# Value products of the grouped-query attention: from column-tiled fp32 matmuls to full-array one-pass matmuls with split operands

## The chip, the cores and the metric

The kernel runs on one core of one Trainium2 chip. The metric is the device time of one execution in microseconds. Lower is better. Three runs of the kernel before gave 1745.05 to 1748.7 us, with a median of 1747.95 us.

## The reference, cut to what matters

One inference step of a two-layer trunk for 512 latent and 128 context tokens of width 1024. Layer 1 is grouped-query attention: 16 query heads, 4 key/value heads of width 64. Latent queries read 512 latent and 128 cached context keys in one softmax, and context queries read the 128 context keys alone.

```python
def one(qblk):
    s = jnp.einsum('bhgqd,bhkd->bhgqk', qblk, k).astype(jnp.float32) * scale
    p = jax.nn.softmax(s, axis=-1).astype(v.dtype)
    return jnp.einsum('bhgqk,bhkd->bhgqd', p, v)
...
k_all = jnp.concatenate([k, k_ctx], axis=2)
v_all = jnp.concatenate([v, v_ctx], axis=2)
o = block_attention(q.reshape(b, GQA_KV_HEADS, GQA_GROUP, n, HEAD_DIM), k_all, v_all)
```

The change concerns the last einsum, p times v.

## The kernel before, in words

Activations lie feature-major: 8 tiles of 128 features by 640 tokens (`NT`, latents first). The big products are made in float32r, a one-pass format of TensorE: each operand is split into a high part (a rounding copy on ACT) and a low part (source minus high part, on DVE or POOL, function `split`), and three matmuls, low-high, high-low and high-high, add up in PSUM (`step`, line 153, tile `mm`). Weights come through `weights` (tiles `ws`, then `wh` and `wl`, lines 111 and 112). `helper` picks DVE or POOL for the subtraction: a table `WPOOL` says, by stage, that every n-th goes to POOL. It held `mix0` alone, so in the stage `mix1`, which is layer 1's attention, all weight splits were DVE's.

`layer1` is that stage. After the k and q projections of the first heads, `tokens_major` makes v with tokens on partitions (tile `tm` in PSUM, copied to `v` by ACT and DVE in turn), and then `pipeline` runs over 72 units: for each of 8 head pairs m, four blocks of 128 queries times two heads e, and one unit for the context queries (`context_unit`, tiles with `ctx` in the name). A unit of `units_of` has these steps:

- scores: four float32r matmuls of 320 columns into tile `gs` (lines 1259 and 1260)
- exps (in `soft`): row maximum on DVE (`mx`, 1011), times the query's norm `rq` (1013), exponential with sum on ACT (1017, tile `gp`)
- norm (in `soft`): reciprocal and product with it on DVE (1022, 1025)
- turn: five transposes of 128 by 128 on TensorE into two PSUM banks (`gpt`, 1268)
- gather: copies of the two banks to SBUF, 256 columns on DVE (1272) and 384 on ACT (1273), tile `gpy`
- values, once for both heads of a pair: ten fp32 matmuls into tile `gpo` (1279), head 0 to PSUM partitions 0 to 63 and head 1 to 64 to 127, then one ACT copy to `gao` (1281)

A step's lag sets how far it runs behind: norm and turn one unit behind the scores, gather and values two. Behind each step `fill.some(rate)` lays matmuls of the q projections of later heads and, from m = 5, of the first half of the output projection, so TensorE has work while a softmax runs. The engines run their own queues in order; the order in them is set by the framework's scheduler from a timeline of its own, with the attention's steps ahead in priority.

## Time and profile before

| what | us |
|---|---|
| median of three runs | 1747.95 |
| the profiled execution | 1748.81 |
| its span, first to last instruction | 1747.0 |
| TensorE busy, of the span | 1672.7 |
| VectorE busy | 1277.5 |
| ScalarE busy | 722.8 |
| GpSimd busy | 206.2 |
| the attention units, first maximum to the last value products | 985 to 1222 |

The profiled execution lasts 1.8 us longer than its span, and 0.9 us longer than the median. Busy time of an engine counts each moment once. In the trace an fp32 matmul or transpose may show as more than one record, and neighbours on one engine overlap a little, since the next starts before the last has written.

### The profile page before, as it was taken

To read this page: it belongs to the slowest core of one execution; us is meant where nothing else is said; L and a number is where in the kernel's file an instruction comes from. 1 tells how busy PE (TensorE), PEld (TensorE's weight loads), DVE (VectorE), ACT (ScalarE), POOL (GpSimd) and SP (SyncE) were. 2 spreads that over 40 slices of the span, in tenths; PEclk is the share of its full clock that TensorE was granted. 3 is DMA by queue.
4 is the path that set the end of the run, shared out by engine and by line. 5 is a ranking of instruction groups with operands and counts; after the bars stand their busy time and mean duration, and the time that the engine had idled before them with its cause. 6 is when DMAs were issued, how large, how long until landed. Compare 5 with 4: busy or idle time off the path is not lost.

```text
span 1747.0 us, 33431 instructions
## 1 busy us (share of the span) xinstructions
PE 1672.7 (96%) x13142; PEld 1573.8 (90%) x13142; DVE 1277.5 (73%) x2877; ACT 722.8 (41%) x1599; POOL 206.2 (12%) x475
## 2 busy tenths in 40 slices
PE   8978899989999999999999999999999999999997
PEld 6867777879899999999998788878899999999997
DVE  5899954765899989997557988875775644663654
ACT  4443254454533322332335566754453322331342
POOL 2134441310200000000003311000110000000001
PEclk8988998999999999999999999999999999999998
DMA  8623223233154555444232200110212222222222
GB/s 314 207 91 130 98 86 99 80 101 97 55 175 155 159 169 183 148 149 131 69 120 89 66 20 19 35 67 22 73 61 74 85 73 73 73 66 93 72 64 72
DMA packets 68014, 175.22 MB, mean 100 GB/s; under 512 B 7920, under 2 KB 9744, under 8 KB 66832
## 3 DMA queue, kind: packets, MB, share of 16 engines
q1 hardware_dynamic: 67024, 171.48, 30.2%
q8 instruction: 103, 1.69, 0.4%
q0 software_dynamic: 832, 1.60, 0.3%
q14 instruction: 55, 0.45, 0.1%
HBM read 165.71 MB, written 7.34 MB: 99 GB/s over the span
## 4 chain that ended last, share of the span: by engine, by line
PE 81%; DVE 12%; DMA 3%; ACT 2%; issue 2%; POOL 0%; SPq 0%; ACTq 0%; DVEq 0%; POOLq 0%
PE mm L153 65%; PE gpo L1279 3%; PE gpt L1268 2%; DVE junk L316 1%; DVE wa L316 1%; PE gs L1259 1%; DMA wa<-in_ada_wt_dram 1%; DVE wl L112 1%; PE gs L1260 1%; PE napo L1076 1%; DVE eb L847 1%; PE ss L410 1%; PE go L949 1%; DVE ea L841 1%; DMA x<-in_xT_dram 1%
## 5 line engine op out<-in xcount | busy, mean ns | idle before, releaser
L153 PE MATMUL mm<-hh,wl 128*128 128x320 f32 x2080 | 651.7, 315 | 5.3 <-DVE x L488 1.0
L153 PE MATMUL mm<-hl,wh 128*128 128x320 f32 x2080 | 648.4, 312 | 0.0
L153 PE MATMUL mm<-hh,wh 128*128 128x320 f32 x2080 | 642.0, 312 | 0.0
L111 ACT CAST wh<-ws 128x512 fp32r<-128x512 f32 x376 | 228.8, 615 | 443.0 <-PE mm L153 404.0
L153 PEld LDWEIGHTS mm<-hh,wl 128*128 128x128 f32 x2080 | 394.6, 190 | 15.6 <-issue 5.9
L153 PEld LDWEIGHTS mm<-hl,wh 128*128 128x128 f32 x2080 | 395.4, 190 | 2.9 <-DVE h L445 1.2
L153 PEld LDWEIGHTS mm<-hh,wh 128*128 128x128 f32 x2080 | 393.3, 190 | 0.9 <-issue 0.3
L112 DVE TENSOR_TENSOR wl<-ws,wh 128x512 fp32r<-128x512 f32 x348 | 240.2, 693 | 159.3 <-ACT wh L111 158.4
L153 PE MATMUL mm<-glo,wh 128*128 128x320 f32 x704 | 217.0, 309 | 0.0
L153 PE MATMUL mm<-ghi,wh 128*128 128x320 f32 x704 | 216.7, 309 | 0.0
L153 PE MATMUL mm<-ghi,wl 128*128 128x320 f32 x704 | 215.8, 309 | 0.0
L488 DVE SCALAR_TENSOR_TENSOR x<-mm,mod,x 128x192 f32<-128x192 f32 (+2 forms) x240 | 96.8, 435 | 93.4 <-PE mm L153 92.6
L153 PEld LDWEIGHTS mm<-ghi,wl 128*128 128x128 f32 x704 | 131.7, 188 | 0.9 <-issue 0.9
L153 PEld LDWEIGHTS mm<-glo,wh 128*128 128x128 f32 x704 | 132.2, 188 | 0.0
L153 PEld LDWEIGHTS mm<-ghi,wh 128*128 128x128 f32 x704 | 132.0, 188 | 0.1
L316 DVE SCALAR_TENSOR_TENSOR junk<-wa,sb 128x512 f32<-128x512 f32 x160 | 115.6, 727 | 7.5 <-DMA wa<-in_ada_wt_dram 7.2
L316 DVE SCALAR_TENSOR_TENSOR wa<-wa,sb 128x512 f32<-128x512 f32 x160 | 117.7, 742 | 0.3
L522 POOL MEMSET u<- 128x1 f32 x88 | 8.9, 103 | 766.3 <-DVE gate L515 432.3
L525 ACT COPY u<-mm 128x320 f32<-128x320 f32 x88 | 37.8, 432 | 88.0 <-PE mm L153 83.1
L592 PE MATMUL tm<-wl,hh 128*128 128x256 f32 x200 | 58.6, 297 | 9.8 <-ACT v L601 7.0
L1011 DVE TENSOR_REDUCE mx<-gs 128x1 f32<-128x640 f32 x64 | 52.5, 821 | 16.6 <-PE gs L1260 16.0
L1017 ACT ACTIVATE gp<-gs,mx,rq 128x640 f32<-128x640 f32 x64 | 57.1, 892 | 9.5 <-DVE mx L1013 5.1
(302 smaller groups left out, 2480.7 us busy)
## 6 DMA issues: line engine op xcount, KB each, us to landing
ws<-in_wu_dram SPq DMA_DIRECT2D x88, 512.0 KB, 3.2
wa<-in_ada_wt_dram SPq DMA_DIRECT2D x160, 256.0 KB, 3.3
ws<-in_wd_dram SPq DMA_DIRECT2D x32, 448.0 KB, 3.2
aw<-in_ada_w_dram SPq DMA_DIRECT2D x8, 1024.0 KB, 15.7
ws<-in_w_ab_dram SPq DMA_DIRECT2D x16, 512.0 KB, 4.2
ws<-in_wd_dram SPq DMA_DIRECT2D x16, 512.0 KB, 3.7
x<-in_xT_dram SPq DMA_DIRECT2D x16, 320.0 KB, 5.5
ws<-in_w_gqa_dram SPq DMA_DIRECT2D x10, 512.0 KB, 3.9
```

The source lines that it names most:

```text
L111: nc.scalar.copy(hi, src)
L112: eng.tensor_tensor(lo, src, hi, ALU.subtract)
L153: nc.tensor.matmul(ps, x, y[:, s], start=st, stop=sp_)
L316: nc.vector.scalar_tensor_tensor(w if v else junk, w, 1.0, cs[v, j], ALU.mult, ALU.mult, accum_out=acc[:, k, v, j:j + 1])
L410: nc.tensor.matmul(ps[0:rows, c:c + 2], part[:, t], onesd, start=True, stop=True)
L488: nc.vector.scalar_tensor_tensor(x[:, b:e], ps[:, b - HN * h:e - HN * h], gate[:, v, m:m + 1], old[:, b:e], ALU.mult, ALU.add)
L525: nc.scalar.copy(u[:, 1:321], ps)
L592: nc.tensor.matmul(ps, hh[:, s], wlo, start=(k == 0), stop=False)
L1011: nc.vector.tensor_reduce(mx[:, 0:n], s, axis, ALU.max, negate=True)
L1017: nc.scalar.activation(dst, src, AF.Exp, bias=mx[:, i:i + 1], accum_out=sm[:, i:i + 1], **kw)
L1268: nc.tensor.transpose(dst, u["p"][0][:, 128 * t:128 * t + 128], ident)
L1279: nc.tensor.matmul(po[64 * f:64 * f + 64, 0:128], vs[t][:, 64 * kv:64 * kv + 64], mates[f]["x"][:, 128 * t:128 * t + 128], start=(t == 0), ...
```

## The change

The value products become float32r matmuls on the whole array. Each token tile of v is kept as high and low part side by side (`gvs`, 64 columns each, so one key/value head is a stationary operand of 128 columns). The transposed probabilities of both heads of a pair are split into high (`hi`, two ACT copies per unit) and low (`lo`, two DVE subtractions per unit). For each of five token tiles two matmuls of 256 columns, 128 for each head, add into one bank: rows 0 to 63 hold the high part of v times p, rows 64 to 127 the low part. A new helper, `weighted`, copies the lower half out on ACT (`gpl`) and adds it to the upper half with two DVE additions. The product with the reciprocal (norm) moves from DVE to POOL for the latent units. `WPOOL` gives POOL every second weight split of `mix1`. Buffers: `gpy` holds one pair instead of two, `ctxp` one unit in this stage, and `adarow` and `kx` move to another pool.

```diff
+                if take:
+                    take(t, ps)
+                    yield
+                    continue
...
-                kx = sp.tile([P, CTX], F32, tag="kx", name="kx")
+                kx = T("kx", "kx", n=CTX, bufs=2)
...
-                nc.vector.tensor_scalar_mul(w, w, sm[:, i:i + 1])
+                (scaler or nc.vector).tensor_scalar_mul(w, w, sm[:, i:i + 1])
...
+        def take(t, src):
+            w = T("gvs", "gvs", F32R, n=512, bufs=6)
+            hi, lo = (w.rearrange("p (g i d) -> p i g d", g=4, i=2)[:, i] for i in range(2))
+            src = src.rearrange("p (g d) -> p g d", g=4)
+            nc.scalar.copy(hi, src)
+            nc.vector.tensor_tensor(lo, src, hi, ALU.subtract)
+            vs.append(w.rearrange("p (g n) -> p g n", g=4))
...
+        def weighted(ot, s, kv, pairs):
+
+            po = P1("gpo", "po")[:, 0:256]
+            n = len(pairs)
+            for t, (v, hi, lo) in enumerate(pairs):
+                nc.tensor.matmul(po, v[:, kv, :], lo, start=(t == 0), stop=False)
+                nc.tensor.matmul(po, v[:, kv, :], hi, start=False, stop=(t == n - 1))
+            low = T("gpl", "gpl", n=256, bufs=1)[0:64]
+            nc.scalar.copy(low, po[64:128])
+            for e in range(2):
+                c = slice(128 * e, 128 * e + 128)
+                nc.vector.tensor_tensor(ot[64 * e:64 * e + 64, s], po[0:64, c], low[:, c], ALU.add)
...
                 def gather():
-                    u["x"] = y = T("gpy", "gpy", bufs=4)
-                    nc.vector.tensor_copy(y[:, 0:256], u["pt"][0][:, 0:256])
-                    nc.scalar.copy(y[:, 256:640], u["pt"][1][:, 0:384])
+                    if e == 0:
+                        u["x"] = [T("gpy", "gpy", F32R, n=2 * NT, bufs=2).rearrange("p (e n) -> p e n", e=2) for _ in range(2)]
+                    hi, lo = (y[:, e] for y in mates[0]["x"])
+                    for w, pt in ((slice(0, 256), u["pt"][0][:, 0:256]), (slice(256, 640), u["pt"][1][:, 0:384])):
+                        nc.scalar.copy(hi[:, w], pt)
+                        nc.vector.tensor_tensor(lo[:, w], pt, hi[:, w], ALU.subtract)
...
-                    for t in range(5):
-                        for f in range(2):
-                            nc.tensor.matmul(po[64 * f:64 * f + 64, 0:128], vs[t][:, 64 * kv:64 * kv + 64],
-                                             mates[f]["x"][:, 128 * t:128 * t + 128], start=(t == 0), stop=(t == 4))
-                    nc.scalar.copy(ot[:, s], po[:, 0:128])
+                    hi, lo = mates[0]["x"]
+                    cols = [slice(128 * t, 128 * t + 128) for t in range(5)]
+                    weighted(ot, s, kv, [(vs[t], hi[:, :, c], lo[:, :, c]) for t, c in enumerate(cols)])
...
-WPOOL = {'mix0': 2}
+WPOOL = {'mix0': 2, 'mix1': 2}
```

TensorE's queue at the value products of the 27th of the 32 pairs, in the kernel before (`gpt` is a transpose, `gpo` a value product, `gs` scores, `gvc` the cached values):

```order
L1279 MATMUL gpo<-gpy,v 64x128
L1268 MATMUL gpt<-ident,gp 128x128
L1279 MATMUL gpo<-gpy,v 64x128
L1268 MATMUL gpt<-ident,gp 128x128
L1279 MATMUL gpo<-gpy,v 64x128 x3
L1259 MATMUL gs<-gkk,q 128x320
L1260 MATMUL gs<-gkl,q 128x320
L1259 MATMUL gs<-gkk,q 128x320
L1260 MATMUL gs<-gkl,q 128x320
L1268 MATMUL gpt<-ident,gp 128x128 x3
L1279 MATMUL gpo<-gpy,v 64x128 x3
L1279 MATMUL gpo<-gpy,gvc 64x128 x2
```

The same pair in the kernel with the change (1271 is a product with the low part of p, 1272 with the high part, 1303 a transpose; two more products follow):

```order
L1271 MATMUL gpo<-gpy,gvs 128x256
L1303 MATMUL gpt<-ident,gp 128x128
L1272 MATMUL gpo<-gpy,gvs 128x256
L1303 MATMUL gpt<-ident,gp 128x128
L1271 MATMUL gpo<-gpy,gvs 128x256
L1272 MATMUL gpo<-gpy,gvs 128x256
L1303 MATMUL gpt<-ident,gp 128x128 x2
L1271 MATMUL gpo<-gpy,gvs 128x256
L1303 MATMUL gpt<-ident,gp 128x128
L1272 MATMUL gpo<-gpy,gvs 128x256
L1271 MATMUL gpo<-gpy,gvs 128x256
L1272 MATMUL gpo<-gpy,gvs 128x256
```

The value products still stand among the transposes of the next unit, but all of them now use 128 columns of the array instead of 64, and each streams 256 columns.

DVE's queue late in the attention, in the kernel before (`mx` is the maximum, `sm` the reciprocal, `x` a residual of the output projection):

```order
L1272 COPY gpy<-gpt 128x256
L1022 RECIPROCAL sm<-sm 128x1
L1025 TENSOR_SCALAR gp<-gp,sm 128x640
L1011 TENSOR_REDUCE mx<-gs 128x1
L1013 TENSOR_TENSOR mx<-mx,rq 128x1
L1011 TENSOR_REDUCE mx<-gs 128x1
L1272 COPY gpy<-gpt 128x256
L1022 RECIPROCAL sm<-sm 128x1
L1013 TENSOR_TENSOR mx<-mx,rq 128x1
```

The same stretch with the change (1311 is a subtraction of gather, 1277 an addition of `weighted`, 1015, 1017 and 1026 the lines 1011, 1013 and 1022 of before):

```order
L1026 RECIPROCAL sm<-sm 128x1
L1017 TENSOR_TENSOR mx<-mx,rq 128x1
L1015 TENSOR_REDUCE mx<-gs 128x1
L1017 TENSOR_TENSOR mx<-mx,rq 128x1
L1026 RECIPROCAL sm<-sm 128x1
L1311 TENSOR_TENSOR gpy<-gpt,gpy 128x256
L1311 TENSOR_TENSOR gpy<-gpt,gpy 128x384
L1015 TENSOR_REDUCE mx<-gs 128x1
L1277 TENSOR_TENSOR gao<-gpo,gpl 64x128 x2
```

The product with the reciprocal is gone from DVE (it stands in POOL's queue now), so a reciprocal, which releases POOL, is followed at once by other DVE work, here by the small product `mx`; two subtractions stand where a copy stood.

## Rows read from the trace of the kernel before

**Rows 1.** The page: the span, and each engine's busy time in it.

```profile
span 1747.0 us, 33431 instructions
...
PE 1672.7 (96%) x13142; PEld 1573.8 (90%) x13142; DVE 1277.5 (73%) x2877; ACT 722.8 (41%) x1599; POOL 206.2 (12%) x475
```

**Rows 2.** Windows over the attention: us, each engine's busy us, clock, DMA share, GB/s.

```profile
1102.00:1142.00 40.00, 40.00 (x362) 32.95 (x361) 34.88 (x93) 27.01 (x65) 6.41 (x4) 1.00 0.20 65
...
1182.00:1222.00 40.00, 40.00 (x298) 32.20 (x298) 22.08 (x59) 16.86 (x42) 0.00 (x0) 1.00 0.06 21
sum 237.00, PE 233.62 PEld 196.07 DVE 189.56 ACT 145.98 POOL 23.36; mean PE 38.94 PEld 32.68 DVE 31.59 ACT 24.33 POOL 3.89
```

**Rows 3.** The chain that ended last, 985 to 1222 us, by line.

```profile
by line: PE mm L153 28.6%; PE gpo L1279 22.9%; PE gpt L1268 17.3%; PE gs L1259 8.9%; PE gs L1260 7.1%; DVE mx L1011 1.7%; DMA ws<-in_w_gqa_dram 1.4%; PE gst L1175 1.3%; PE ctxo L1116 1.1%; DVE wl L112 1.1%; PE ctxpt L1107 1.0%; issue 0.9%; 
```

**Rows 4.** Timeline of TensorE: start, us. Value products in one piece.

```profile
1087.80 0.31 PE L153 MATMUL mm<-hh,wh 128*128 128x320 f32 x1
1088.04 1.09 PE L1279 MATMUL gpo<-gpy,v 128*64 128x128 f32 x16
...
1089.29 0.55 PE L1268 MATMUL gpt<-ident,gp 128*128 128x128 f32 x3
```

**Rows 5.** Timeline of TensorE: value products broken up by transposes.

```profile
1101.60 0.27 PE L1268 MATMUL gpt<-ident,gp 128*128 128x128 f32 x1
1101.81 0.65 PE L1279 MATMUL gpo<-gpy,v 128*64 128x128 f32 x6
...
1104.07 0.42 PE L1259 MATMUL gs<-gkk,q 128*128 128x320 f32 x1
```

**Rows 6.** Timeline of TensorE: float32r matmuls of 256 columns, first and 14th of a run.

```profile
965.81 0.28 PE L593 MATMUL tm<-wh,hl 128*128 128x256 f32 x1
...
967.34 0.28 PE L594 MATMUL tm<-wh,hh 128*128 128x256 f32 x1
```

**Rows 7.** Longest waits, 985 to 1222 us: who, for whom, us, times, longest.

```profile
PEld gpt L1268 <- issue: 8.6, 50, 0.2
PEld gpo L1279 <- issue: 8.1, 46, 0.2
```

**Rows 8.** Groups of DVE by shape, 985 to 1222 us: busy, mean ns, idle before.

```profile
L1025 DVE TENSOR_SCALAR gp<-gp,sm 128x640 f32<-128x640 f32 x64 | 36.3, 568 | 0.4
L1272 DVE COPY gpy<-gpt 128x256 f32<-128x256 f32 x64 | 26.7, 417 | 12.5 <-PE gpt L1268 12.0
L112 DVE TENSOR_TENSOR wl<-ws,wh 128x512 fp32r<-128x512 f32 x24 | 17.4, 734 | 1.1 <-ACT wh L111 1.0
L1013 DVE TENSOR_TENSOR mx<-mx,rq 128x1 f32<-128x1 f32 x64 | 14.1, 221 | 0.2
...
L488 DVE SCALAR_TENSOR_TENSOR x<-mm,mod,x 128x320 f32<-128x320 f32 x7 | 3.8, 547 | 2.1 <-PE mm L153 2.1
...
L488 DVE SCALAR_TENSOR_TENSOR x<-mm,mod,x 128x128 f32<-128x128 f32 x6 | 2.1, 342 | 0.0
...
L1013 DVE TENSOR_TENSOR mx<-mx,rq 128x2 f32<-128x2 f32 x8 | 1.2, 154 | 0.1
```

**Rows 9.** Timeline of POOL and DVE: start, us.

```profile
1088.06 1.72 POOL L1181 TENSOR_TENSOR gx<-gx,cosT 128x512 f32<-128x512 f32 x1
1088.57 1.23 DVE L1013 TENSOR_TENSOR mx<-mx,rq 128x1 f32<-128x1 f32 x1
```

**Rows 10.** Groups of POOL by shape, whole span.

```profile
L701 POOL CAST kl<-kl 64x320 fp32r<-64x320 f32 x16 | 8.2, 514 | 25.9 <-DVE kl L699 25.4
...
L941 POOL TENSOR_TENSOR qd<-qd,kqg 128x640 f32<-128x640 f32 x4 | 6.1, 1545 | 7.4 <-ACT qd L830 7.4
```

**Rows 11.** Groups of ACT by shape, 985 to 1222 us.

```profile
L1111 ACT COPY ctxx<-ctxpt 128x256 f32<-128x256 f32 x8 | 3.0, 378 | 3.9 <-PE ctxpt L1107 3.9
```

**Rows 12.** Windows of the first conv FFN, where DVE is busiest; columns as in Rows 2.

```profile
680.00:720.00 40.00, 40.00 (x275) 40.00 (x274) 39.09 (x95) 14.81 (x34) 1.12 (x15) 1.00 0.52 169
...
sum 240.00, PE 239.42 PEld 239.16 DVE 224.51 ACT 73.93 POOL 4.41; mean PE 39.90 PEld 39.86 DVE 37.42 ACT 12.32 POOL 0.73
```

More of the change, by code (lines that the diff above doesn't have):

```diff
@@ L286, in spread_modulation @@
             nc.tensor.matmul(ps[j:j + 32, 0:128 * n], siluc[:, r, :], w[:, 128 * n * r:128 * n * (r + 1)], start=(r < 4), stop=(r >= 4))
-        row = sp.tile([P, 256], F32, tag="adarow", name="adarow")[:, 0:128 * n]
+        row = T("adarow", "adarow", n=256, bufs=2)[:, 0:128 * n]
         nc.scalar.copy(row, ps[:, 0:128 * n])
@@ L575, in conv_ffn, with tokens_major @@
         return into_norm(xs, gate(), lambda done: run(products(ws[0:KD - 3], g, done, kinds, n)), ws, g, n, final=final)
-    def tokens_major(src, n, H, vs, tag, bufs=None, out=None):
+    def tokens_major(src, n, H, vs, tag, bufs=None, out=None, take=None):
         per = 512 // n
-        for t in range(5):
+        for t in range(0 if take else 5):
             if t % per == 0:
@@ L1119, in view @@
         def view():
-            t = T("ctxp", "ctxp", n=256, bufs=2)
+            t = T("ctxp", "ctxp", n=256, bufs=1 if scale is not None else 2)
             return [t[:, 0:128], t[:, 128:256]]
@@ L1236, in layer1, with latents @@
         together([a["w_gqa"][c] for c in range(3)], H, kq_done, make)
-        v = []
-        run(tokens_major(a["w_gv"], 256, H, v, "gv", 3))
-        nc.gpsimd.dma_start(o["gqa_v"], v[4][:, 0:256])
+        vs = []
+        def take(t, src):
[5 more added lines that the diff above has]
+            vs.append(w.rearrange("p (g n) -> p g n", g=4))
+        def latents(t, ps):
+            take(t, ps)
+            if t == 4:
+                x = T("gvc", "gvc", n=256, bufs=1)
+                nc.scalar.copy(x, ps)
+                nc.gpsimd.dma_start(o["gqa_v"], x)
+        run(tokens_major(a["w_gv"], 256, H, None, None, take=latents))
         vc = T("gvc", "gvc", n=256, bufs=1)
         nc.sync.dma_start(vc, a["gqa_vc"])
-        vs = v[0:4] + [vc]
+        take(None, vc)
+        vx = vs.pop(4)
         outs = []
+        def weighted(ot, s, kv, pairs):
[9 more added lines that the diff above has]
+                nc.vector.tensor_tensor(ot[64 * e:64 * e + 64, s], po[0:64, c], low[:, c], ALU.add)
         def units_of(m, q, r):
@@ L1291, in units_of, with gather @@
                 units += [unit(b, e, mates) for e in range(2)]
-            units.append(context_unit(q, [KX[kv]] * 2, [KXL[kv]] * 2, slice(0, CTX), r[:, 4, :],
-                                      lambda e: v[4][:, 64 * kv:64 * kv + 64], ot))
+            u = context_unit(q, [KX[kv]] * 2, [KXL[kv]] * 2, slice(0, CTX), r[:, 4, :], None, ot)
+            def gather():
+                u["x"] = hi, lo = [T("ctxx", "ctxx", F32R, n=256, bufs=2) for _ in range(2)]
+                pt = u["pt"][:, 0:256]
+                nc.scalar.copy(hi, pt)
+                nc.vector.tensor_tensor(lo, pt, hi, ALU.subtract)
+            u.update(gather=gather, values=lambda: weighted(ot, slice(LAT, NT), kv, [(vx, *u["x"])]))
+            units.append(u)
             return units
```

6 lines of the change are left out of this document (2 added, 4 removed).

## The prediction, made before the change was timed

> **What bounds the kernel now.** I read the page first: TensorE is busy for 96% of the span, DVE for 73%, ACT and POOL for far less [rows 1]. But a busy TensorE is not one at its peak, and the change touches one stage only, so next come the windows over that stage, 985 to 1222 us. There TensorE is busy 233.6 of 237 us at full clock, DVE 189.6, ACT 146.0, POOL 23.4. The stage has two halves: while q projections are still made, DVE is busy 34.9 of 40 us (87%); at the end, 22.1 of 40 [rows 2]. The chain that ended last runs through TensorE almost without a break: 22.9% of the stage is on the value products, 17.3% on transposes, and the two DVE lines named have 2.8% [rows 3]. So TensorE sets the pace now, and while projections are made DVE stands close behind. The reader should keep that in mind: what TensorE is spared counts only until DVE is full.
>
> **TensorE: what is removed.** The value products take 22.9% of 237 us in the chain, 54.3 us, and those of the context units 1.1%, 2.6 us [rows 3]. Two pieces of the timeline show what this is made of. In one piece, the 20 records of a pair (ten matmuls, two records each) last from 1088.04 to 1089.29, 1.25 us, and the first starts 0.24 us after the last `mm`, whose own 320 columns take 0.133 at 2.4 GHz [rows 4]. Broken up by transposes, the same 20 records with three transposes between them last from 1101.81 to 1104.07, 2.26 us [rows 5]. Every change between 128 columns of the array and 64 columns costs: the weight loader idles 46 times for 8.1 us before value products and 50 times for 8.6 us before transposes, for nothing that the profile can name [rows 7].
>
> **TensorE: what is added.** 32 pairs of ten and 8 context units of two float32r matmuls of 256 columns. The trace has that shape in `tm`: 14 starts in 1.53 us, 0.118 us each [rows 6]. 336 of them make 39.6 us. All use the whole array, so the gaps at a change of columns should go.
>
> The streaming alone is hardly cheaper: 1.25 us in one piece against 1.18, 0.07 for each of 32 pairs, some 2 us. The gain is the switches. 54.3 + 2.6 - 39.6 = 17.3 us, which has the gaps on leaving, and the gaps on entering, 8.1 us named "issue" and some 2 more under other names: about 27 us. Lower bound 17 (no entry gap goes), upper bound 35 (every entry costs 0.2 us).
>
> The Trainium skill (FP8 and Floating Point Precision, TensorE Precision Notes) says that true fp32 takes four passes through the array. By it the ten matmuls of a pair would stream four times 128 columns each, 2.13 us at 2.4 GHz, and the streaming alone would give 30 us; the trace does not bear that out, since a whole pair takes 1.25 us [rows 4].
>
> **DVE: what is removed and added.** Removed: the product with the reciprocal, 36.3 us; the copy of 256 columns, 26.7; and 12 of the 24 weight splits, at 734 ns 8.8 us [rows 8]. Together 71.8. Added: per unit a subtraction of 256 and one of 384 columns from PSUM. The first I take as the copy of that size, 417 ns, the second as 560, between that plus 128 columns (about 0.13 us) and the 547 ns of 320 columns plus 64 more. 64 units: 62.5 us. Per pair and context unit two additions of 128 columns on 64 partitions: 342 ns is the nearest row (three operands), I take 310, 80 of them 24.8 us. Eight context subtractions, 3.3. Together 90.6, net +19. Neighbours overlap, so +12 is the lower bound.
>
> **DVE: what POOL costs it.** The product with the reciprocal goes to POOL, 64 times. No row has it. A one-input cast of 320 columns takes 514 ns there, a two-input product of 640 columns 1545 [rows 10]; I take 1.0 us, being one-input, with 0.9 and 1.55 as bounds. POOL then works 64 to 100 us more, plus some 15 for weight splits: 100 to 140 of 237, so it is no bound itself. But look at what happens to DVE beside it: `mx`, a product of one column, takes 154 ns in its undisturbed form and 221 in the mean [rows 8], and 1.23 us when it meets a POOL instruction, ending as that does [rows 9]. 64 x 0.067 = 4.3 us are lost on `mx` in 23.4 us of POOL work. 75 to 117 us more of it would cost 14 to 22 us by that ratio. Two things make it less: POOL's new instruction is shorter, and the maximum before `mx` often covers it. The order shown above has both cases: a reciprocal, which releases POOL, with `mx` right behind it, and one with two subtractions behind it. I take 10, bounds 0 and 35.
>
> The Trainium skill (SBUF — State Buffer, Who interferes with whom) says that a DVE instruction with two SBUF inputs contends with a POOL instruction that reads SBUF, and that whichever comes second blocks fully. The rows on `mx` agree. This rule speaks against the change; its worst case is the rival "POOL blocks DVE" below, whose price is worked from rows.
>
> **The sum.** TensorE needs 237 - 27 = 210 us, DVE 189.6 + 19 + 10 = 219. So DVE becomes the bound. How full can it run? In the first conv FFN it is busy 39.1 of 40 us at best and 224.5 of 240 over six windows [rows 12]; I take the middle, 95.5%. 219 / 0.955 = 229 us, 8 us less than 237. ACT gets 64 more casts of 256 columns at 378 ns [rows 11], 24 us on 146: 72%, no bound.
>
> Costed at nothing: the split of v while `tm` matmuls fill TensorE (five short pairs; 2 us if uncovered); the later copy-out of the value products, since `gpo` is next written a pair, some 6 us, later; moving `adarow` and `kx`, which shifts the order in layer 0 a little (3 us either way); eight weight splits on POOL at both ends of the stage, 1 us or so. The one loaded `gvc` buffer now waits for the new v to be written out, and the weight loads queued behind it on SP wait too; the first unit's whole softmax lies between, so I take 0, and 3 us if the weights are late.
>
> The sum is made against the profiled execution: 1747.0 us of span and 1.8 around it, 1748.8 in all, 0.9 above the median of the runs. 8 us less than the median is 1740.
>
> **The rivals.**
> - **TensorE stays the bound, the gain comes whole.** DVE instructions cost less back to back than their durations, and POOL's short ones are covered. For it: DVE's load at the end is 55%; against it: 87% earlier [rows 2]. 27 to 35 us less: about 1719.
> - **No change that can be measured.** The transposes' banks are now freed only by ACT's cast and then DVE's subtraction in a row, and TensorE's queue waits at the next transpose. 8 us over 72 units is 0.11 us each, less than one of the idle gaps in rows 7; a wait of that size leaves 1748.
> - **POOL blocks DVE, slower.** Place: `mx`, the weight splits and the small rotary products on DVE while POOL multiplies by the reciprocal. With POOL at 1.55 us an instruction and every second unit hit, 35 us: DVE needs 244, at 95.5% 255 us, 18 more: 1766. It decides from 18 us on, where DVE's need passes 95.5% of 237. The middle of this case is 12 more, 1760. For it: rows 9; against it: half of the reciprocals have a maximum or subtractions behind them.
>
> **How the numbers follow.** A measurement of this kernel can tell about 0.2%, 3.5 us, from no change. DVE-bound with 8 us won: 0.42, own range 1724 (no blocking, DVE at 97%) to 1750. Whole gain: 0.22. No change: 0.13. POOL blocks DVE: 0.23. Faster: 0.37 of the first and 0.22, 0.59. Same: 0.04 and 0.13, 0.17. Slower: 0.24. The range leaves out a tenth at each end, the better half of the whole gain and the worse half of the blocking: 1717 to 1759.
>
> **What would show it.** Right, step by step: value products at 0.118 us start to start, with no gap before or behind them; DVE busy above 90% of the stage, and a chain that now runs through DVE's subtractions and maxima; the reciprocal's product on POOL at about 1 us; `mx` with a mean well above 221 ns. Wrong: DVE busy below 85% with TensorE still in the chain (whole gain), or TensorE waiting before transposes for POOL or for the subtraction; `mx` with a mean near 700 ns would be the blocking. A difference outside 900 to 1310 us would mean that the shifted order of layer 0, which I cost at nothing, decides.

## The result, and the profile after

The kernel after takes 1798.72 us in the median of four runs (1797.15 to 1802.93), the kernel before 1747.86. The ratio is 1.0298, with a 95% interval from 1.0277 to 1.0319: 51 us slower, where the prediction said 8 us faster and a range that ended at 1759.

The page of after has 49.9 us more span. TensorE's share of it falls, and only POOL's, which got the product with the reciprocal, is clearly larger (compare [rows 1]):

```profile
span 1796.9 us, 33219 instructions
...
PE 1667.8 (93%) x12806; PEld 1588.9 (88%) x12806; DVE 1309.6 (73%) x2949; ACT 749.8 (42%) x1667; POOL 349.9 (19%) x559
```

Where the time lies is read from four marks in the two traces: the first instruction on a tile `u` (layer 0's attention is over), the first and the last row maximum of a latent unit in layer 1, and the end.

```
us          first u   first max   last max      end   attention (last - first max)
before        414.4       984.8     1202.0   1747.0   217.2
after         419.6       995.6     1253.2   1796.9   257.6
```

Of 49.9 us the attention has 40.4, the part up to the first `u` 5.2, the way from there to the first maximum 5.6, and what follows is 1.3 shorter. The windows over the attention of after, from 985 to 1262 us, to be held against [rows 2] (columns: us, then busy us of PE, PEld, DVE, ACT, POOL, the granted clock, DMA):

```profile
1025.00:1065.00 40.00, 34.62 (x264) 31.07 (x262) 31.18 (x89) 25.45 (x63) 23.45 (x15) 0.96 0.06 21
...
1145.00:1185.00 40.00, 30.60 (x242) 28.23 (x240) 34.69 (x93) 28.16 (x66) 25.07 (x16) 0.96 0.14 45
...
sum 277.00, PE 225.49 PEld 205.95 DVE 221.88 ACT 175.58 POOL 161.57; mean PE 32.21 PEld 29.42 DVE 31.70 ACT 25.08 POOL 23.08
```

The reader is to see that nobody is full. TensorE is busy 225.5 of 277 us, where it was busy 233.6 of 237; DVE 221.9, 80%; ACT and POOL less. DVE's work is what the prediction had summed up, 219 us. It has these 277 us for it, where the prediction gave it 229.

The clock column shows a second difference. Between the first and the last maximum of before the granted clock was full throughout. In after it was at the lower level, 1.2 GHz, for 20.5 of the 257.6 us (0.96 in the mean), and four of the five falls come right behind idle stretches of TensorE of 1.7 to 3.0 us. Around the fall at 1148.5 us a matmul of 320 columns takes 0.267 us from start to start, and 0.148 once the clock is back. TensorE was busy in nearly all of those 20 us. At full clock their work would have taken little more than half the time, so the falls are worth at most some 10 of the 40 us: an estimate, from these rows. No run separates them, since they come with the idling.

The chain that ended last, from 995 to 1273 us, is no longer TensorE's (compare [rows 3]); it names many lines on three engines and none with more than 8.2%:

```profile
by line: PE mm L153 8.2%; DVE gpy L1311 3.8%; DVE mx L1015 3.1%; PE gpt L1303 2.8%; PE gpo L1271 2.7%; issue 2.5%; ACT gp L1021 2.3%; PE gpo L1272 2.2%; DVE gao L1277 1.6%; PE gs L1294 1.5%; ACT gpy L1310 1.4%; DVE x L488 1.4%; PE gs L1295 
```

So the engines wait for each other, and the longest waits from 985 to 1270 us say for what (who, on which line, for whom: us in total, times, longest; POOL's own wait for its input, 76.0 us, is left out):

```profile
PEld gs L1294 <- ACT gp L1021: 26.0, 26, 4.9
ACT gp L1021 <- PE gpt L1303: 21.2, 9, 3.7
PE gs L1294 <- ACT gp L1021: 20.2, 21, 4.7
ACT gpy L1310 <- PE gpt L1303: 17.7, 19, 2.9
DVE sm L1026 <- ACT gp L1021: 15.5, 21, 2.0
...
ACT gpy L1310 <- PE gpo L1271: 9.5, 8, 2.5
...
PEld gpo L1271 <- DVE gpy L1311: 7.8, 6, 2.8
PE gpt L1303 <- DVE gpy L1311: 7.5, 11, 1.7
...
PE gpo L1271 <- DVE gpy L1311: 6.5, 6, 2.6
```

It goes round: TensorE's scores (1294) wait for the bank that the exponential (1021) reads, the exponential stands in ACT's queue behind a cast (1310) that waits for transposes (1303), and waits for transposes itself, 21.2 us in all, since it writes one of three `gp` buffers that the transposes read; and transposes and value products (1271) wait for DVE's subtraction (1311). One more tie shows: a pair's first cast waits for the value products of the pair before, 9.5 us, because `gpy` has room for one pair only. One turn of it, from the timeline of after (start, us, engine, and in brackets how long the engine had been idle and for whom), TensorE first, then ACT, DVE and POOL:

```profile
1145.10 0.71 PE L1303 MATMUL gpt<-ident,gp 128*128 128x128 f32 x5
1146.34 0.36 PE L1271 MATMUL gpo<-ctxx,gvs 128*128 128x256 f32 x1 [0.53 <-DVE gao L1277]
1146.53 0.28 PE L1272 MATMUL gpo<-ctxx,gvs 128*128 128x256 f32 x1
1148.55 0.90 PE L1303 MATMUL gpt<-ident,gp 128*128 128x128 f32 x3 [1.74 <-DVE gpy L1311]
...
1146.05 0.62 ACT L111 CAST wh<-ws 128x512 fp32r<-128x512 f32 x1
1146.55 0.49 ACT L1310 CAST gpy<-gpt 128x384 fp32r<-128x384 f32 x1
...
1146.23 0.73 DVE L1183 STREAM_SHUFFLE gy<-gx 128x512 f32<-128x512 f32 x1
1146.86 1.16 DVE L1017 TENSOR_TENSOR mx<-mx,rq 128x1 f32<-128x1 f32 x1
1147.95 0.55 DVE L1311 TENSOR_TENSOR gpy<-gpt,gpy 128x384 fp32r<-128x384 f32 x1
...
1146.74 1.26 POOL L112 TENSOR_TENSOR wl<-ws,wh 128x512 fp32r<-128x512 f32 x1 [1.47 <-ACT wh L111]
```

Transposes are written by 1145.8. Their cast stands behind a weight cast on ACT, to 1147.0; the subtraction behind a shuffle and behind `mx`, which takes 1.16 us instead of 0.15 because POOL is splitting a weight. Only at 1148.5 is the bank free, and TensorE, whose queue goes on with the next unit's transposes, has stood still for 1.74 us. The clock falls at the same moment: the three transposes that follow start 0.21 to 0.27 us apart, the five before 0.109.

The value products themselves do what was said: 0.12 us from start to start, and scores follow without a gap.

```profile
1121.20 0.28 PE L1271 MATMUL gpo<-gpy,gvs 128*128 128x256 f32 x1
1121.32 0.28 PE L1272 MATMUL gpo<-gpy,gvs 128*128 128x256 f32 x1
1121.43 0.31 PE L1294 MATMUL gs<-gkk,q 128*128 128x320 f32 x1
```

### The profile page after: what moved, and what is told of

Read it like the earlier page. It is cut to its first block, busy times and chain, and to the rows that moved or that the text cites. A ratio compares the mean times of both kernels' runs of the same rounds, so it can differ in the third digit from the quotient of the medians.

```text
span 1796.9 us, 33219 instructions
## 1 busy us (share of the span) xinstructions
PE 1667.8 (93%) x12806; PEld 1588.9 (88%) x12806; DVE 1309.6 (73%) x2949; ACT 749.8 (42%) x1667; POOL 349.9 (19%) x559
## 5 line engine op out<-in xcount | busy, mean ns | idle before, releaser
L153 PEld LDWEIGHTS mm<-hh,wh 128*128 128x128 f32 x2080 | 397.3, 192 | 0.6 <-issue 0.2
L112 DVE TENSOR_TENSOR wl<-ws,wh 128x512 fp32r<-128x512 f32 x328 | 226.3, 692 | 156.5 <-ACT wh L111 155.4
L1029 POOL TENSOR_SCALAR gp<-gp,sm 128x640 f32<-128x640 f32 x64 | 122.8, 1921 | 96.8 <-DVE sm L1026 76.0
L316 DVE SCALAR_TENSOR_TENSOR junk<-wa,sb 128x512 f32<-128x512 f32 x160 | 119.4, 752 | 9.3 <-DMA wa<-in_ada_wt_dram 6.9
L112 POOL TENSOR_TENSOR wl<-ws,wh 128x512 fp32r<-128x512 f32 x48 | 68.1, 1422 | 258.1 <-ACT wh L111 162.2
```

What stands on the lines that cost most here:

```text
L112: eng.tensor_tensor(lo, src, hi, ALU.subtract)
L153: nc.tensor.matmul(ps, x, y[:, s], start=st, stop=sp_)
L316: nc.vector.scalar_tensor_tensor(w if v else junk, w, 1.0, cs[v, j], ALU.mult, ALU.mult, accum_out=acc[:, k, v, j:j + 1])
L1029: (scaler or nc.vector).tensor_scalar_mul(w, w, sm[:, i:i + 1])
```

## The experiments

Each ratio is to the kernel before on the same chip. "Attention" is as above, first to last maximum, of the profiled run. The names of the theories changed from one set of runs to the next as some fell; each expectation says what its letters mean. The framework orders the queues anew for every kernel, so each number also holds what that order happens to bring. Where the text gives a difference to the kernel after in us, it is one of medians from different chips, on which the kernel before had medians from 1746.95 to 1750.63 us. Worked out from the ratios, these differences come out 1 to 4 us larger (19.9 instead of 16 for the additions), and each is known to within 5 or 6 us.

### Which of the moved pieces costs

**The product with the reciprocal, back on DVE** (e1_norm_dve):

```diff
-                return soft(u, 1, AX.XY, lambda: [T("gp", "gp", bufs=3)], r[:, b, e:e + 1], nc.gpsimd)
+                return soft(u, 1, AX.XY, lambda: [T("gp", "gp", bufs=3)], r[:, b, e:e + 1])
```

> The changed kernel with one part undone: the product with the reciprocal is DVE's again. Theory P (the product takes 1.89 us on POOL against 0.57 on DVE, and the 1.3 us more lie on the chain from scores to transposes of every latent unit, so TensorE waits): most of the 51 us come back, 1735 to 1762 us, and TensorE's waits for the exponential before scores shrink from 46 us to under 15. Theory G (the gather in series, ACT's cast and then DVE's subtraction, holds the transposes' banks): 1785 us or more, the waits of transposes and value products for the subtraction stay near 28 us. Theory W (weight splits on POOL): no change, 1795 to 1802.

1799.79 us, 1.0291 [1.0274, 1.0308], as after. **No weight split of `mix1` on POOL** (e2_no_wpool):

```diff
-WPOOL = {'mix0': 2, 'mix1': 2}
+WPOOL = {'mix0': 2}
```

> The changed kernel with the weight splits of the attention stage all on DVE again, as before the change. Theory W (the twelve splits of 1.28 us each in POOL's queue delay the products with the reciprocal that stand behind them, and the early ones delay the first products of the stage): 1770 us or less. Theory P: 5 to 15 us come back, since POOL's queue is 15 us shorter but each product still takes 1.89 us: 1784 to 1794. Theory G: 1795 to 1802.

1790.20 us, 1.0243 [1.0224, 1.0263]: 8.5 us less than after. **Both edits** (e3_values_only):

> Both undone: product with the reciprocal and weight splits on DVE. What is left of the change is the value products with their splits and additions. Theory P: TensorE has its 17 to 35 us, DVE has 36 us of products and 9 us of splits more than in the changed kernel, 226 of 237 us before any wait, so DVE is the bound: 1745 to 1765 us. Theory G: 1785 us or more.

1789.45 us, 1.0243 [1.0213, 1.0273]. And the reverse, **the kernel before with only that product on POOL** (e4_before_norm_pool; its diff is the argument `nc.gpsimd` and the `scaler` of `soft`):

> The kernel before with one part of the change alone: the product with the reciprocal of the latent units on POOL. Theory P: 1775 to 1800 us, nearly the whole loss without any of the new value products. Theory G and theory W: within 10 us of the kernel before, or faster, since DVE is spared 36 us.

1744.94 us in ten runs, 0.9982 [0.9967, 0.9997]. Theory P, my first, falls: POOL's latency costs nothing in either kernel. The weight splits on POOL are a small part, and what is left after both are undone, 42 us over before, belongs to the value products and their gather.

### The gather

**Without the subtractions** (f2_one_pair; f2_two_pairs has `bufs=2` there):

```diff
-                        u["x"] = [T("gpy", "gpy", F32R, n=2 * NT, bufs=2).rearrange("p (e n) -> p e n", e=2) for _ in range(2)]
-                    hi, lo = (y[:, e] for y in mates[0]["x"])
+                        u["x"] = [T("gpy", "gpy", F32R, n=2 * NT, bufs=1).rearrange("p (e n) -> p e n", e=2) for _ in range(1)]
+                    hi = mates[0]["x"][0][:, e]
...
-                        nc.vector.tensor_tensor(lo[:, w], pt, hi[:, w], ALU.subtract)
...
-                    hi, lo = mates[0]["x"]
+                    hi, lo = mates[0]["x"][0:1] * 2
```

> The kernel after, with the low part of the probabilities left out: ACT's two casts of a unit stay, DVE's two subtractions go, and the value products multiply the high part twice, so that TensorE has the same matmuls; one pair of probabilities is held, as in the kernel after. The output lacks the low part. Theory G (the transposes' banks come free only after a cast on ACT and then a subtraction on DVE, and the in-order queues of TensorE, ACT and DVE wait on each other): the stage falls from 257.6 us by 25 to 45, time 1755 to 1775. Theory D (DVE's load of 62 us of subtractions, wherever they stand): the same size, which the other runs of this call tell from G. Theory B (the split probabilities of one pair only are held): no more than 10 us better, 1788 or above. Theory E (the copy of the lower half and the two additions behind the value products): 1788 or above.

> The same without the low part, with buffers for two pairs of the high part. Theory B: at least 20 us under the run with one pair. Theories G, D, E: within 6 us of it.

1757.43 us, 1.0053 [1.0036, 1.0070], and 1755.65 us, 1.0045 [1.0028, 1.0063]. The subtractions carry 41 us; a second pair of buffers, where there are none, nothing. Theory B falls as far as that goes; a second pair beside the subtractions, where the first cast waits 9.5 us for it, was not tried, and neither was a fourth `gp` buffer.

**The kernel before with its gather in series** (f3_before_serial), and **with the same work on DVE but no bank held by it** (f6_before_load):

```diff
-                    nc.vector.tensor_copy(y[:, 0:256], u["pt"][0][:, 0:256])
-                    nc.scalar.copy(y[:, 256:640], u["pt"][1][:, 0:384])
+                    junk = N("junk")
+                    for w, pt in ((slice(0, 256), u["pt"][0][:, 0:256]), (slice(256, 640), u["pt"][1][:, 0:384])):
+                        nc.scalar.copy(y[:, w], pt)
+                        nc.vector.tensor_tensor(junk[:, w], pt, y[:, w], ALU.subtract)
```

```diff
                     nc.scalar.copy(y[:, 256:640], u["pt"][1][:, 0:384])
+                    nc.vector.tensor_tensor(N("junk")[:, 256:640], y[:, 256:640], y[:, 256:640], ALU.subtract)
```

> The kernel before, its value products and all its output kept, but the probabilities gathered as the kernel after does it: ACT copies both banks, then DVE subtracts from each bank what ACT has copied, into a tile that nobody reads. DVE gets 64 subtractions of 256 and 384 columns and loses the copy of 256, about 36 us more on 198 of 237. Theory G: slower by 20 to 45 us, 1767 to 1792. Theory D: slower only as far as DVE is full, by 0 to 15 us, and the same as the next run. Theories B and E: within 6 us of before.

> The kernel before with the same extra load on DVE but no bank held by it: behind the copies of a unit DVE subtracts 384 columns of the copy in SBUF from themselves, into a tile that nobody reads. Theory G: at least 15 us faster than the run before this one, within 10 us of the kernel before. Theory D: as slow as the run before this one, within 5 us. Theories B and E: within 6 us of before.

1757.42 us, 1.0048 [1.0033, 1.0063], and 1759.82 us, 1.0059 [1.0044, 1.0074]. Both are 8 to 10 us slower, and the one can't be told from the other: theory G as I had priced it (20 to 45 us for the series alone) falls, and both came out as theory D, DVE's load, had them. (In the profiled runs the attention takes 233.0 and 231.5 us, 14 to 16 more than in that of before, while the first `u` comes 6 to 7 us earlier.) The sums of their windows from 985 to 1225 us, f3 and then f6, show DVE at 88% in both, with TensorE at 93 and 96%:

```profile
sum 240.00, PE 222.47 PEld 186.34 DVE 210.65 ACT 159.28 POOL 21.26; mean PE 37.08 PEld 31.06 DVE 35.11 ACT 26.55 POOL 3.54
```

```profile
sum 240.00, PE 231.05 PEld 190.84 DVE 210.75 ACT 141.41 POOL 21.08; mean PE 38.51 PEld 31.81 DVE 35.13 ACT 23.57 POOL 3.51
```

So DVE can have 211 us of work in 240 and cost 10. The kernel after has 222 us of it and costs 40 in the attention.

**Without the additions** (f4_no_addition), **with tiny subtractions** (f5_tiny_sub) and **with subtractions that no value product reads** (f7_sub_unread):

```diff
-            low = T("gpl", "gpl", n=256, bufs=1)[0:64]
-            nc.scalar.copy(low, po[64:128])
...
-                nc.vector.tensor_tensor(ot[64 * e:64 * e + 64, s], po[0:64, c], low[:, c], ALU.add)
+                nc.scalar.copy(ot[64 * e:64 * e + 64, s], po[0:64, c])
```

```diff
                         nc.scalar.copy(hi[:, w], pt)
+                        nc.vector.tensor_tensor(small("tiny"), pt[:, 0:2], hi[:, w][:, 0:2], ALU.subtract)
```

```diff
-                    weighted(ot, s, kv, [(vs[t], hi[:, :, c], lo[:, :, c]) for t, c in enumerate(cols)])
+                    weighted(ot, s, kv, [(vs[t], hi[:, :, c], hi[:, :, c]) for t, c in enumerate(cols)])
```

> The kernel after, with the lower half of the values' columns left out of the output: behind the value products ACT copies the upper half out in two pieces, and the copy of the lower half and DVE's two additions are gone. DVE loses 22 of its 206 us in the stage. Theory S (what costs is DVE's work that stands in the circle of one unit: subtraction, addition, reciprocal, each behind a wait for another engine): faster than the kernel after by 12 to 25 us, 1774 to 1787. Theory H (the transposes' banks wait for DVE's queue, whatever stands in it) and theory V (the value products wait for the subtraction): within 8 us of the kernel after, 1791 or above.

> The kernel after without the low part, as in the run that returned 41 us (the high part multiplied twice), but behind each of ACT's casts DVE subtracts two columns of the same bank, 128 a row in all: a bank is again free only when DVE's queue has come to it, with almost no work there, and no value product waits for DVE. Theory H: 1785 or above. Theory S: 1757 to 1767, within 10 us of the run without subtractions. Theory V: the same as S.

> The kernel after with all its subtractions, but the value products of the latent units read the high part twice and the low part never: the same work on every engine, only TensorE no longer waits for the subtraction before a value product. Theory V: 1757 to 1772, most of the 41 us. Theories S and H: 1790 or above, within 9 us of the kernel after.

1782.53 us, 1.0184 [1.0158, 1.0210]; 1762.35 us, 1.0072 [1.0054, 1.0089]; 1776.04 us, 1.0152 [1.0127, 1.0178]. The additions carry 16 us. Tiny subtractions come out 5 us over none, within the noise of the two, so it is not DVE's queue as such that holds the banks (theory H falls). And the largest single piece is one that no sum of loads can have: 23 us go when the same subtraction is made and no value product reads it. That lies between the ranges of theory V (1757 to 1772) and of S and H (1790 or above). In the profiled run of f7_sub_unread the value products have no wait for the subtraction left, the transposes still have theirs (7.5 us in after):

```profile
PE gs L1294 <- ACT gp L1021: 14.7, 10, 4.8
PE gpt L1303 <- DVE gpy L1311: 14.5, 15, 2.4
```

The edit loosens a second tie with the first, though. A low part that nobody reads leaves its buffer early: in f7 the first cast of 9 of 31 pairs begins before the last value product of the pair before has ended, by up to 5.6 us, and in after none does. So the 23 us hold the wait of the value products and the single pair of buffers together, and no run parts the two.

### The order of layer 0

**The kernel before with `adarow` and `kx` in the phase's buffers** (g1_before_pools):

```diff
-        row = sp.tile([P, 256], F32, tag="adarow", name="adarow")[:, 0:128 * n]
+        row = T("adarow", "adarow", n=256, bufs=2)[:, 0:128 * n]
...
-                kx = sp.tile([P, CTX], F32, tag="kx", name="kx")
+                kx = T("kx", "kx", n=CTX, bufs=2)
```

> The kernel before with only the two small tiles adarow and kx taken from the phase's own buffers, as in the kernel after; no instruction is added or left out, but the static order of the program shifts from layer 0 on. Theory O (the shifted order costs what layer 0 and the entry show in the kernel after): 1755 to 1762, with layer 0 ending at 417 us or later. Rival (that part is another execution of the same, as I had costed it): 1745 to 1752.

1755.26 us in ten runs, 1.0032 [1.0019, 1.0045], with the attention at 217.0 us as before: the moved tiles cost 4.6 us (3 to 8 by the ratio), though they hold the same data. In the traces the first `u` comes at 407 to 414 us in all five kernels with those tiles as before, and at 417 to 425 in all with the tiles moved.

### One set of banks?

Over the 64 latent units the trace also gives the mean time from a unit's first transpose to the end of its gather, and from there to the next unit's first transpose:

```
us                                  to the end of the gather    then to the next unit's first transpose
before                                     2.66                     0.87
f6_before_load                             2.58                     1.16
f2_one_pair                                2.75                     0.79
f5_tiny_sub                                3.21                     0.32
f3_before_serial                           3.67                     0.09
f4_no_addition                             3.84                     0.09
f7_sub_unread                              4.04                    -0.25
after                                      4.20                    -0.04
```

Where a subtraction of full size reads the banks, the next unit's transposes begin in the mean when the gather ends: the set of two banks is hardly ever free as a whole. (Each bank by itself lies free for 1.0 us in the mean in after, between its subtraction and the next transposes into it, and for 2.2 in before.) The table adds up the period and does not say what sets it. 63 steps of 4.16 us make 262, the attention of after and little more; 63 of 3.53 make 222 for the kernel before. To see whether a second set helps, the transposes were given one bank for each unit in turn, with the fifth block and the value products in a third, and the context units' transposes and the tile `gst` moved into these banks too (h2_two_banks); with the subtractions left out too (h4_banks_no_sub); and with the one set freed by raw copies as in the kernel before, cast and subtraction then made from SBUF on ACT and POOL (h3_raw):

```diff
-                    u["pt"] = [P1("gpt") for _ in range(2)]
+                    j = next(turns) % 2
+                    u["pt"] = pt2[j], pt2[2][:, 128 * j:128 * j + 128]
...
-            po = P1("gpo", "po")[:, 0:256]
+            po = pt2[2][:, 256:512]
...
+        pt2 += [P1("gpt"), P1("gpt"), P1("gpo", "po")]
```

```diff
-                        nc.scalar.copy(hi[:, w], pt)
-                        nc.vector.tensor_tensor(lo[:, w], pt, hi[:, w], ALU.subtract)
+                    raw = N("raw")
+                    nc.vector.tensor_copy(raw[:, 0:256], u["pt"][0][:, 0:256])
+                    nc.scalar.copy(raw[:, 256:640], u["pt"][1][:, 0:384])
+                    nc.scalar.copy(hi, raw)
+                    nc.gpsimd.tensor_tensor(lo, raw, hi, ALU.subtract)
```

> The kernel after with two sets of columns for the transposed probabilities instead of one: four blocks of a unit in one bank of its own, the fifth and the value products' 256 columns share a third bank. No instruction is added; a unit's gather is cast and subtraction of 512 and of 128 columns. Theory K (the stage is 64 times the hold of the one set, 4.2 us): the next unit's transposes start before the gather ends, the stage falls from 257.6 us to 220 to 238, time 1760 to 1780. Theory Q (DVE's load and the order of its queue): within 8 us of the kernel after, 1790 or above.

> The kernel after with one set of banks that is freed as in the kernel before, by a copy of 256 columns on DVE and one of 384 on ACT side by side, into SBUF; from there ACT makes the cast of all 640 columns and POOL the subtraction, and the product with the reciprocal is back on DVE. Work is added on ACT (one cast of 640 columns a unit). Theory K: the hold falls to 2.7 us or so and the stage to 225 to 240, time 1762 to 1782, with ACT at 85 to 90%. Theory Q: DVE has 203 us to do in the stage, as in the kernel after, so 1785 or above.

> Two sets of columns as in the first run of this call, without the low part of the probabilities and its subtractions (the high part multiplied twice, buffers for two pairs). Nothing but ACT's casts stands between transposes and value products. If TensorE's gain of 23 us (215.9 us of busy time against 233.5) can be had, the stage falls below that of the kernel before, 217.2 us, to 200 to 212, time 1738 to 1750; if the waits for the exponential on ACT are the limit, it stays at 217 to 222, time 1753 to 1760.

All three are slower than the kernel after, and no theory had that, except that theory Q's range for h3_raw has no upper end: 1854.53 us, 1.0615 [1.0590, 1.0640]; 1838.02, 1.0520 [1.0495, 1.0546]; 1810.48, 1.0362 [1.0335, 1.0390]. They don't answer the question. The waits of h2_two_banks show why (985 to 1305 us; line 1304 are the transposes, 1271 the value products, 1311 the casts, 1312 the subtractions):

```profile
ACT gpy L1311 <- PE gpo L1271: 38.3, 27, 3.7
ACT gpy L1311 <- PE gpo L1304: 37.5, 25, 3.7
...
PEld gpo L1304 <- DVE gpy L1312: 19.3, 19, 2.9
```

The fifth block's transpose now waits for what else goes on in the shared third bank, and the cast for the transposes there: new waits in the same circle, worth more than the old ones. The raw copy doesn't shorten the time on the banks: from a unit's first transpose to the end of its two copies the trace of h3_raw has 4.4 us in the mean, against 4.20 in after, since the copies stand in the same queues. And it makes the way of a unit longer: POOL's subtraction waits 128.8 us for ACT's cast. Whether a second set of banks without a shared one would help wasn't tried; in this stage every bank is in use.

### TensorE's part by itself

**No subtraction and no addition** (i1_no_sub_no_add, the edits of f2_one_pair and f4_no_addition together), **the new matmuls in the old stage** (i2_tensor_only), and **fp32 value products on the whole array** (i3_fp32_whole), the values doubled in `gvs` and `WPOOL`, the small tiles and the context units' gather as before. From the last two (i2, then i3):

```diff
-            low = T("gpl", "gpl", n=256, bufs=1)[0:64]
...
+            nc.scalar.copy(ot[:, s], po[:, 0:128])
...
+                    nc.vector.tensor_copy(hi[:, 0:256], u["pt"][0][:, 0:256])
+                    nc.scalar.copy(hi[:, 256:640], u["pt"][1][:, 0:384])
```

```diff
+            for t, (v, y) in enumerate(pairs):
+                nc.tensor.matmul(po, v[:, kv, :], y, start=(t == 0), stop=(t == n - 1))
+            for e in range(2):
+                d = slice(64 * e, 64 * e + 64)
+                nc.scalar.copy(ot[d, s], po[d, 128 * e:128 * e + 128])
```

> The kernel after without the low part of the probabilities (the high part multiplied twice) and without the lower half of the values' columns in the output: no subtraction of the latent units and no addition on DVE, ACT's casts and two copies out remain. If the pieces add up (41 us for the subtractions, 16 for the additions), 1739 to 1748, with the stage at 204 to 212 us; if TensorE's in-order queue waits for ACT's casts instead, no more than 8 us under the run without subtractions: 1749 to 1758.

> The matmuls of the kernel after in the stage of the kernel before: the probabilities gathered as there, by a copy of 256 columns on DVE and one of 384 on ACT side by side (rounded to float32r, the high part multiplied twice), one copy out of 128 columns for a pair; the product with the reciprocal stays on POOL, which alone changed nothing. The low part and one unit's output of each pair are left out. If the 23 us of TensorE can be had: stage 190 to 203 us, time 1730 to 1742 with layer 0 as in the kernel after. If waits for the exponential on ACT or another bound take its place: 1743 to 1756.

> The whole output, with fp32 value products on the whole array: the values of a head stand twice side by side in 128 columns, and five fp32 matmuls of a pair's 256 columns take the place of ten of 128 on half the columns; two copies of 64 partitions take the result out. Gather and small tiles as in the kernel before, the product with the reciprocal on POOL. No split of the probabilities, no subtraction, no addition. If an fp32 matmul of 256 columns on the whole array takes two records of 0.118 us (as twenty records of ten matmuls in rows 4 suggest): value products fall to 1.2 us a pair without the gaps at a change of columns, 1718 to 1732. If the two halves of the array were working side by side in the kernel before and the fp32 matmul needs four passes: 2.1 us or more a pair, 1745 to 1765.

1752.35 us, 1.0024 [1.0009, 1.0039], attention 212.5; 1754.69 us, 1.0048 [1.0030, 1.0066], attention 215.6; 1759.27 us, 1.0059 [1.0040, 1.0078], attention 225.5. The two pieces of i1 don't add up: 46 us under after, not 41 and 16. And i2, with TensorE's new matmuls and nothing else of the gather, takes the time of the kernel before with the tiles moved, 1.0048 against 1.0032. Its sum from 985 to 1225 us:

```profile
sum 240.00, PE 218.56 PEld 206.43 DVE 184.38 ACT 152.34 POOL 163.04; mean PE 36.43 PEld 34.40 DVE 30.73 ACT 25.39 POOL 27.17
```

TensorE is spared work, 218.6 us in 240 where it was busy 233.6 in 237 [rows 2], and stands idle 21 us instead of 3. Its clock was at the lower level for 10 of the 215.6 us. No engine is full; TensorE's longest wait in total is that of the scores for the exponential, 7.8 us. Which of them would have to go for the gain to be seen stays open.

The fp32 run shows something else. Its timeline, six records of three matmuls of 256 columns:

```profile
1085.10 1.46 PE L1271 MATMUL gpo<-gpy,gvs 128*128 128x256 f32 x6
```

with one record at 0.38 us by the group

```profile
L1271 PE MATMUL gpo<-gpy,gvs 128*128 128x256 f32 x313 | 80.5, 381 | 0.1
```

is (1.46 - 0.38) / 5 = 0.216 us from start to start, at full clock; a matmul has two, 0.43 us, four times the 0.107 us of 256 columns at 2.4 GHz. A pair takes 2.16 us, against 1.25 in [rows 4]. So the ten matmuls of the kernel before ran two at a time, one in each half of the array's columns, and its trace bears that out: the 20 records of [rows 4] start in twos, 6 ns apart, with 0.109 us from one two to the next.

## Why the prediction was wrong

**The sum of loads as the bound: the step that failed.** "DVE becomes the bound. How full can it run?", with 95.5% taken from the conv FFN [rows 12]. DVE's work came out near the forecast of 219 us: 220.4 from the first maximum to the last value product of a latent pair, in 279.5 us. That was partly luck: the 10 us for POOL's blocking came out at some 4, and some 6 us more of DVE's other work (`x`, `nt`, `ny`) came to lie in the longer stage. Its fill was not near, 79% against 95.5. In the FFN nobody waits for DVE in the middle of a unit. Here each unit now goes ACT, DVE, TensorE, ACT, DVE behind its transposes, in queues whose order is fixed. f7_sub_unread shows that it isn't the load: the same instructions on every engine, and 23 us less when the value products no longer wait for the subtraction and its buffer is free at once. The prediction's own sign for this, "TensorE waiting before transposes for POOL or for the subtraction", is what the trace of after has. f6_before_load is the other side of it: DVE at 88% without such a wait costs 10 us.

**"No change that can be measured" named the mechanism and priced it wrongly.** It had the banks freed by a cast and then a subtraction in a row, TensorE waiting at the next transpose, and gave that 0.11 us a unit, from the idle gaps of [rows 7], which have nothing to do with it. In the account of the table, the banks are held 1.54 us longer a unit (2.66 to 4.20), of which the free time behind it gave 0.91 (0.87 to -0.04); the rest, 0.63 us in each of 63 steps, is the 40 us of the attention. What a unit holds and what is free until the next could have been read from the timeline of before; the prediction read neither. It isn't the series alone, though: in the kernel before it costs 8 us (f3_before_serial). It becomes 40 with value products that read the low part and so hold its buffer (23 us), additions behind them (16) and weight splits on POOL that stop `mx` in front of a subtraction (8.5; five such stops in the trace of after, of 3.5 us together, so most of it has no cause shown), each removed alone from the kernel after; they overlap, as i1_no_sub_no_add shows, so they are no shares of a sum.

**TensorE: 27 us.** The work was saved about as said: without subtractions (f2_one_pair) TensorE is busy 216.5 us in 240, against 210 forecast, with 37 more projection matmuls (532 against 495 records of `mm` up to 20 us behind the last maximum), 5 us, laid into the stage. The gaps at a change of columns went as said: before value products the weight loader idles without a named reason 2 times for 0.6 us in after, where [rows 7] has 46 times and 8.1 us. The time was not saved: i2_tensor_only and i1_no_sub_no_add leave 20 us of it idle. So the rival "TensorE stays the bound, the gain comes whole" came true in none of the orders that were run, even with DVE relieved.

**The clock**, taken as full from [rows 2] and costed at nothing, was 0.96 in the attention of after: at most some 10 of its 40 us, as estimated above.

**The four passes.** I wrote that the trace doesn't bear out the Trainium skill (FP8 and Floating Point Precision, TensorE Precision Notes), which has true fp32 take four passes through the array, since a pair takes 1.25 us. That reading was wrong. On the whole array an fp32 matmul of 256 columns takes 0.43 us in i3_fp32_whole, four times its columns: the rule holds, the trace agrees. The sum is not touched by it, since it was made from the chain's shares.

**POOL.** The product with the reciprocal takes 1.9 us, not 1.0, and lies outside my bounds of 0.9 and 1.55, which were taken from a cast and a two-input product:

```profile
L1029 POOL TENSOR_SCALAR gp<-gp,sm 128x640 f32<-128x640 f32 x64 | 122.8, 1921 | 96.8 <-DVE sm L1026 76.0 <-PE ctxpt L1111 3.9 <-DVE mx L1017 3.7
```

It costs nothing all the same (e1 and e4). The 10 us of blocking on DVE came out at some 4: `mx` has a mean of 249 ns against 221, 64 times, and the sums of the rotary products on DVE (`gx`) take 7.2 us instead of 4.8.

```profile
L1017 DVE TENSOR_TENSOR mx<-mx,rq 128x1 f32<-128x1 f32 x64 | 15.8, 249 | 0.6
```

So the rival "POOL blocks DVE" ended on the right side of the kernel before, but not by the mechanism it named: without the reciprocal's product on POOL the time is the same. And the prediction's "The rows on `mx` agree" holds for POOL's two-input products; beside the one-input product most `mx` ran undisturbed (last section).

**Durations** were right where a near row stood: subtractions at 418 and 551 ns (417 and 560 said), additions at 279 (310). **The order of layer 0**, costed at "3 us either way", costs 4.6 us. **Entry**: costed at nothing, 5.6 us between the first `u` and the first maximum in the traces, not tested by itself (in e2 and e3, with the weight splits back on DVE, 1.5 us, each in one execution).

**A version that beats both.** The only one found with the whole output is the kernel before with the product with the reciprocal on POOL, 0.9982 [0.9967, 0.9997]; that is 3 us, no more than the measurement can just tell.

## What to carry to other kernels

A sum of each engine's work is a lower bound. Where a change puts a second engine's instruction between a producer and the bank that it needs again, measure in the trace of before how long a unit holds that bank and how long it then lies free; here the new time came off the free time first, and the rest came to the period. A matmul made faster in a stage whose queues wait for each other can come out as a longer wait and nothing else, as in i2_tensor_only: try the faster matmul alone before paying for it elsewhere. And take a fill of an engine from the stage itself, with its waits, not from one where nobody waits for it.

## What the runs showed of the hardware

A one-input product with a per-row factor of 128x640 fp32 takes 1.9 us on POOL, longer than the two-input product of that size at 1545 ns [rows 10]; on DVE it takes 568 ns [rows 8]. It hardly holds up DVE beside it: of 24 `mx` in after that met nothing else on POOL, 18 took 0.16 us or less, the longest 0.6. Counted in the traces, `mx` instructions that overlap a POOL instruction, by its kind (an `mx` that meets two is counted for both):

```
kernel                 POOL's instruction                 mx that overlap   mean ns
before                 none                                     67            150
before                 two-input product, rotary                 5           1061
e4_before_norm_pool    none                                     37            152
e4_before_norm_pool    one-input product, reciprocal            31            189
e4_before_norm_pool    two-input products, rotary                6            925
```

So it is mostly POOL's two-input instructions that stop an `mx`, not POOL at work. And two fp32 matmuls of 64 columns each, in different halves of the array, ran side by side, their records 6 ns apart: ten of them in 1.25 us where the same products on the whole array take 2.16.
